# A two-block sequence model on one core: the sums behind its seven-product pairs move from POOL to DVE

## The chip, the cores and the metric

The kernel runs on one core of a Trainium2 chip. The metric is the device time of one execution in microseconds (us). The core has a matmul engine (PE, with PEld for its weight loads), a vector engine (DVE), an activation engine (ACT), a general engine (POOL, also called GpSimd) and DMA queues issued from SP. Each engine works through its own list of instructions in order and waits on semaphores of the others.

## The reference, cut to what matters

Two model blocks run one after the other on 512 tokens of width 1024 (and 256 context tokens in the second block), all in float32. The first block (an even and an odd mixer with two feed-forward parts) isn't touched by the change. The second block has two layers (`l`), each with a joint projection of the normalised tokens, three branches (`branch_a` differential attention, `branch_b` a chunked bidirectional recurrence, `branch_c` neighbourhood attention) and a gated merge:

```python
h = rms_norm(x, norm_g) * (1 + scale[:, None]) + shift[:, None]
aq, ak, av, az, bq, bk, bv, bo, bz, bg, cq, ck, cv, cz, gm = split_proj(h @ w_in)
...
g = jax.nn.sigmoid(gm.reshape(gm.shape[:2] + (N_BRANCH, -1)))
return jnp.sum(g * proj, axis=2) @ w_out
```

The gates `gm` are 3072 columns of `h @ w_in`, for 768 tokens in layer 0 and 512 in layer 1. They are where the changed code works.

## The kernel before, in words

**Matmuls in three parts.** A float32 product is made of three products of rounded parts: an operand is split by ACT (`hi`, a copy in the shorter format) and DVE (`lo`, the remainder), and `mm3` issues hi·hi, hi·lo, lo·hi. The normalised tokens stand in two resident tensors, `H` (hi) and `L` (lo). Weights arrive by DMA in `ws`, are split into `wh` by ACT and `wl` by DVE, and wait in three `ws`, four `wh` and four `wl` buffers.

**Seven-product pairs.** Two weight tiles for `gm` are multiplied with the tokens as a 2x2 block product with seven products in place of eight (`pair`, called by `gm_pair`; 12 pairs in each layer, 24 in all). That needs sums of blocks of the weights and of the tokens:

- `wpair` loads the two tiles into `ws` and makes, with four operations of 128x512, `a11-a21` (in place), `s2 = a22-a11` (in the tile `w2`, printed as `w`), `a12-s2` (in place) and `a21+a22` (in place). Between them the parts are split for the matmuls (`put`), so ACT (`wh<-w`) and DVE (`wl<-w,wh`) wait for these sums.
- `halves` runs once in each layer, at its start: for eight row tiles it adds the two parts of the tokens, `H + L`, back to float32 (128x768 in layer 0, 128x512 in layer 1; printed as `s<-H,L`), and then DVE subtracts halves of those (`s<-s`, `s<-s,s`) and splits them.

**What sets the order.** Every instruction is recorded by `Order` and issued by a planner in `flush`. It simulates the engines with costs of its own (`_cost`), takes at each step the instruction that could start first, and prefers the earlier one in the program's order among those that are ready. Its costs know the engine of an operation and nothing of what other engines do at that moment:

```python
if eng == "pool":
    return 146 + (2.1 if op == "tensor_tensor" else 3.3) * size
...
return 95 + size / (1.92 if two else 0.96)
```

Changing an operation's engine thus changes its planned cost, the planned load of two engines, and the order of everything that is planned with it. Block 2 is planned by itself, from the first `s<-H,L` on.

**Around the change.** At a layer's start `norm_lat`/`norm_ctx` write `H` and `L`; the first head of `branch_c` is prepared (`stack`: four ACT copies `s<-s 64x768`, DVE subtractions `s<-s,s 64x768`, DVE casts), and only with it can PE go on from projections to scores. In `attend` of `branch_c` and `branch_a`, DVE scales the exponentials (`s<-s,tn`), which PE then transposes (`P<-C,s`) for the product with the values.

Of the kernel before, what the change touches and what calls it, by code (L numbers as in the profile page):

```python
# [9 lines left out]
F32 = mybir.dt.float32  # L10
# [3 lines left out]
ALU = mybir.AluOpType  # L14
# [496 lines left out]
class Kern:  # L511
# [68 lines left out]
    def wpair(self, srcs):  # L580


        nc = self.nc
        self.n_ += 1
        raw = []
        for i, src in enumerate(srcs):
            st = nc.tile(self.wp, [128, 1088], F32, "wst", self.WST, f"ws{self.n_}_{i}")
            nc.sync.dma_start(out=st[:, :1024], in_=src.rearrange("p k m -> p (k m)"))
            raw.append(st)
        s2 = nc.tile(self.wp, [128, 512], F32, "w2", 1, f"w2{self.n_}")  # L590
        a11, a12, a21, a22 = (raw[i][:, 512 * j:512 * j + 512] for i in range(2) for j in range(2))
        out = {}

        def put(x, names, tags=("whi", "wlo", 1088, 4)):
            self.n_ += 1
            n = 512 * len(names)
            hi = nc.tile(self.wp, [128, tags[2]], F32R, tags[0], tags[3], f"wh{self.n_}")[:, :n]
            lo = nc.tile(self.wp, [128, tags[2]], F32R, tags[1], tags[3], f"wl{self.n_}")[:, :n]
            self.split(hi, lo, x[:, :n])
            for i, a in enumerate(names):  # L600
                out[a] = [y[:, 512 * i:512 * i + 512].rearrange("p (k m) -> p k m", k=4) for y in (hi, lo)]

        sub = lambda o, x, y: nc.gpsimd.tensor_tensor(o, x, y, op=ALU.subtract)
        put(raw[0], ("a11", "a12"))
        sub(a11, a11, a21)
        sub(s2, a22, a11)
        put(s2, ("s2",), ("w2h", "w2l", 512, 1))
        sub(a12, a12, s2)
        put(raw[0], ("s3", "s4"))
        nc.gpsimd.tensor_tensor(a21, a21, a22, op=ALU.add)  # L610
        put(raw[1], ("s1", "a22"))
        return out

# [567 lines left out]
class Block2:  # L1181
# [95 lines left out]
    def halves(self, n):  # L1277

        K, nc = self.K, self.nc
        b = self.tk = {q: [] for q in ("b11", "b21", "b22", "t1", "t2", "t3", "t4")}  # L1280
        for k in range(4):
            for nm, r, c in (("b11", k, 0), ("b21", k + 4, 0), ("b22", k + 4, n)):
                b[nm].append((K.H[:, r, c:c + n], K.L[:, r, c:c + n]))
        self.tn = n
        for k in range(4):
            x, y = self.s(2 * n), self.s(2 * n)
            for a, r in ((x, k), (y, k + 4)):
                nc.gpsimd.tensor_tensor(a, K.H[:, r, :2 * n].bitcast(F32), K.L[:, r, :2 * n].bitcast(F32), op=ALU.add)
            b11, b12, b21, b22 = x[:, :n], x[:, n:], y[:, :n], y[:, n:]
            nc.vector.tensor_tensor(b11, b12, b11, op=ALU.subtract)  # L1290
            nc.vector.tensor_tensor(b12, b22, b12, op=ALU.subtract)
            nc.vector.tensor_tensor(b22, b22, b11, op=ALU.subtract)
            nc.vector.tensor_tensor(b21, b21, b22, op=ALU.subtract)
            for a, names in ((x, ("t1", "t3")), (y, ("t4", "t2"))):
                h, l = self.ysplit(a, 2 * n)
                for i, nm in enumerate(names):
                    b[nm].append((h[:, i * n:i * n + n], l[:, i * n:i * n + n]))
            yield
# [701 lines left out]
```

## Time and profile before

| | |
|---|---|
| three timed runs | 2883.07 us median (2879.26 to 2884.18) |
| profiled execution, its own time | 2883.25 us |
| its span in the profile | 2881.5 us |
| mean granted clock of TensorE | 0.993 |
| PE busy | 2831.4 us (98%) |
| DVE busy | 2057.3 us (71%) |
| ACT busy | 1306.7 us (45%) |
| POOL busy | 393.4 us (14%), 285 instructions |

Busy time is the union of an engine's instructions. The span is the profiled program; the 1.75 us between it and the execution's own time lie around the program. The stretch before the first `s<-H,L` (at 1142 us) is block 1 and its hand-over, the 1740 us behind it are block 2. Since the engines work in order and overlap, a share of 98% on PE means that what is left to win or lose are PE's short idle stretches and the time that it runs at the lower of its two clocks.

### The profile page before, as it was taken

The numbers are of one execution on the slowest core, as the hardware profiler recorded it, in microseconds if no ns is written. First come the engines' busy times: TensorE is split into PE (matmuls) and PEld (weight loads), VectorE is DVE, ScalarE is ACT, GpSimd is POOL, SyncE is SP. The second block draws the span as 40 slices with busy tenths as digits, with TensorE's granted clock in tenths as the row PEclk, the third lists the DMA queues.
The fourth block names the chain that finished last, engine by engine and source line by source line (L and its number), as shares of the span: only waits on it lengthen the run. The fifth ranks groups of instructions, "written<-read, shape, count | busy, mean of one in ns | idle before, by whom it ended". The sixth has DMA issues, their size and how long they took to land. (4 is left out here: it accounts for less than half of the span.)

```text
span 2881.5 us, 42542 instructions
## 1 busy us (share of the span) xinstructions
PE 2831.4 (98%) x16280; PEld 2452.8 (85%) x16280; DVE 2057.3 (71%) x4049; ACT 1306.7 (45%) x2449; POOL 393.4 (14%) x285
## 2 busy tenths in 40 slices
PE   9999999999999999999999999999999999999998
PEld 7888888887888888889899989998878889989887
DVE  7878687478875875855777676575586677787765
ACT  6344234465442443754545453341256554554433
POOL 1010000010100003100211131120210121232201
PEclk9999999999999999999999999999999999999999
DMA  4333433332324423111112132254312222232362
GB/s 171 125 120 124 144 133 110 105 106 80 137 99 145 142 89 118 63 67 57 72 67 71 59 104 92 76 165 164 135 63 94 71 81 71 71 107 96 107 211 92
DMA packets 113245, 302.63 MB, mean 105 GB/s; under 512 B 11657, under 2 KB 25353, under 8 KB 113041
## 3 DMA queue, kind: packets, MB, share of 16 engines
q1 hardware_dynamic: 112896, 299.91, 30.7%
q8 instruction: 128, 2.10, 0.3%
q14 instruction: 77, 0.62, 0.1%
q10 hardware_dynamic: 144, 0.00, 0.0%
HBM read 272.26 MB, written 27.61 MB: 104 GB/s over the span
## 5 line engine op out<-in xcount | busy, mean ns | idle before, releaser
L486 PE MATMUL P<-H,wl 128*128 128x512 f32 (+2 forms) x2648 | 960.9, 363 | 4.0 <-DVE wl L486 4.0
L486 PE MATMUL P<-L,wh 128*128 128x512 f32 (+2 forms) x2648 | 961.2, 363 | 2.5 <-DVE L L486 2.5
L486 PE MATMUL P<-H,wh 128*128 128x512 f32 (+2 forms) x2648 | 960.9, 364 | 1.4 <-ACT H L486 1.4
L486 ACT ACTIVATE wh<-ws 128x1024 fp32r<-128x1024 f32 (+3 forms) x450 | 436.1, 972 | 764.3 <-PE P L486 649.1
L486 DVE TENSOR_TENSOR wl<-ws,wh 128x1024 fp32r<-128x1024 f32 (+3 forms) x450 | 523.3, 1164 | 204.3 <-ACT wh L486 202.4
L486 PEld LDWEIGHTS P<-H,wl 128*128 128x128 f32 x2648 | 500.3, 189 | 82.7 <-DVE wl L486 5.4
L486 PEld LDWEIGHTS P<-L,wh 128*128 128x128 f32 x2648 | 499.6, 189 | 83.3 <-DVE L L486 4.6
L486 PEld LDWEIGHTS P<-H,wh 128*128 128x128 f32 x2648 | 499.0, 188 | 81.4 <-ACT H L486 2.4
L486 PE MATMUL P<-s,wh 128*128 128x256 f32 (+2 forms) x1344 | 330.6, 333 | 0.0
L486 PE MATMUL P<-t,wh 128*128 128x512 f32 x960 | 301.5, 395 | 0.3 <-ACT t L486 0.3
L486 ACT ACTIVATE s<-P 128x512 f32<-128x512 f32 (+3 forms) x416 | 186.6, 482 | 222.9 <-PE P L486 202.7
L486 PE MATMUL P<-s,s 128*128 128x128 f32 (+4 forms) x1576 | 239.1, 293 | 11.9 <-DVE s L486 11.8
L486 PEld LDWEIGHTS P<-s,wh 128*128 128x128 f32 x1344 | 229.6, 189 | 17.6
L486 PEld LDWEIGHTS P<-s,s 128*128 128x128 f32 (+1 forms) x1576 | 212.8, 192 | 28.7 <-issue 10.2
L486 PE MATMUL P<-s,wl 128*128 128x256 f32 (+2 forms) x672 | 222.8, 332 | 2.1 <-DVE wl L486 2.1
L486 PEld LDWEIGHTS P<-t,wh 128*128 128x128 f32 x960 | 180.4, 188 | 43.0 <-ACT t L486 0.6
L486 ACT ACTIVATE s<-s 128x768 f32<-128x768 f32 (+7 forms) x226 | 153.3, 694 | 114.7 <-DVE s L486 97.9
L486 DVE TENSOR_TENSOR s<-s,s 128x512 f32<-128x512 f32 (+8 forms) x200 | 173.9, 875 | 26.2 <-ACT s L486 11.9
L486 PE MATMUL P<-t,wl 128*128 128x512 f32 x480 | 189.8, 395 | 0.0
L486 POOL TENSOR_TENSOR s<-s,s 128x512 f32<-128x512 f32 (+2 forms) x76 | 102.8, 1356 | 582.2 <-DVE s L486 317.7
L486 ACT ACTIVATE s<-P,tn 128x512 f32<-128x512 f32 (+1 forms) x224 | 117.8, 534 | 107.0 <-DVE tn L486 106.9
L486 ACT ACTIVATE t<-t 128x512 f32<-128x512 f32 (+4 forms) x162 | 97.5, 611 | 123.5 <-DVE t L486 122.6
(145 smaller groups left out, 3579.8 us busy)
## 6 DMA issues: line engine op xcount, KB each, us to landing
ws<-in_w2in SPq DMA_DIRECT2D x136, 512.0 KB, 3.3
ws<-in_up SPq DMA_DIRECT2D x88, 512.0 KB, 3.2
wm<-in_w_mod SPq DMA_DIRECT2D x48, 512.0 KB, 4.4
ws<-in_down SPq DMA_DIRECT2D x32, 384.0 KB, 3.1
ws<-in_w2br SPq DMA_DIRECT2D x48, 256.0 KB, 2.7
ws<-in_down SPq DMA_DIRECT2D x32, 320.0 KB, 2.9
ws<-in_w0in SPq DMA_DIRECT2D x18, 512.0 KB, 3.7
gd<-s SPq DMA_DIRECT2D x24, 384.0 KB, 2.9
```

What stands on the lines that cost most here:

```text
L486: o["f"](*o["a"], **o["k"])
```

## The change

The 96 operations of 128x512 in `wpair` and the 16 operations in `halves` (8 of 128x768, 8 of 128x512) are issued on DVE in place of POOL. Nothing else in the source is different; the planner then orders block 2 anew.

```diff
@@ wpair
-        sub = lambda o, x, y: nc.gpsimd.tensor_tensor(o, x, y, op=ALU.subtract)
+        sub = lambda o, x, y: nc.vector.tensor_tensor(o, x, y, op=ALU.subtract)
         put(raw[0], ("a11", "a12"))
         sub(a11, a11, a21)
         sub(s2, a22, a11)
         put(s2, ("s2",), ("w2h", "w2l", 512, 1))
         sub(a12, a12, s2)
         put(raw[0], ("s3", "s4"))
-        nc.gpsimd.tensor_tensor(a21, a21, a22, op=ALU.add)
+        nc.vector.tensor_tensor(a21, a21, a22, op=ALU.add)
         put(raw[1], ("s1", "a22"))
@@ halves
             for a, r in ((x, k), (y, k + 4)):
-                nc.gpsimd.tensor_tensor(a, K.H[:, r, :2 * n].bitcast(F32), K.L[:, r, :2 * n].bitcast(F32), op=ALU.add)
+                nc.vector.tensor_tensor(a, K.H[:, r, :2 * n].bitcast(F32), K.L[:, r, :2 * n].bitcast(F32), op=ALU.add)
```

The order of block 1 is the same on every engine. In block 2 three places on DVE matter here. The first is DVE at the start of layer 0, from the last `L` of the normalised tokens to the first subtractions of `stack` (`s_9672`, `s_9671`); `s_9695` and `s_9696` are the first two row tiles of `halves`, `s_9732` the third.

```order
 L486 SCALAR_TENSOR_TENSOR L<-t_2040,mod_79,H 128x512
+L486 TENSOR_TENSOR s_9695<-H,L 128x768
 L486 TENSOR_TENSOR wl_2064<-ws_2062,wh_2063 128x1024
 L486 TENSOR_TENSOR wl_2067<-ws_2065,wh_2066 128x1024
-L486 TENSOR_TENSOR wl_9799<-ws_9797,wh_9798 128x1024
+L486 TENSOR_TENSOR s_9696<-H,L 128x768
 L486 TENSOR_TENSOR s_9695<-s_9695 128x384
 L486 TENSOR_TENSOR s_9695<-s_9696,s_9695 128x384
+L486 TENSOR_TENSOR s_9696<-s_9696,s_9695 128x384
+L486 TENSOR_TENSOR s_9732<-H,L 128x768
 L486 TENSOR_TENSOR s_9672<-s_9667,s_9672 64x768
 L486 TENSOR_TENSOR s_9671<-s_9669,s_9670 64x768
```

Three of the eight sums stand ahead of `stack`'s subtractions, with one more small subtraction; the split of a later weight tile (`wl_9799`) has moved behind them, and the other five sums come later.

The second place is DVE at the first pair of layer 0, in the middle of a head's attention: `ws_0_10056` and `ws_1_10057` are the two weight tiles, `w_10058` is `s2`, `tn` are row statistics, `s_9973` and `s_9976` the exponentials being scaled.

```order
+L486 TENSOR_TENSOR ws_0_10056<-ws_0_10056,ws_1_10057 128x512
 L486 RECIPROCAL tn_9971<-tn_9971 128x2
+L486 TENSOR_TENSOR ws_1_10057<-ws_1_10057 128x512
 L486 TENSOR_SCALAR s_9973<-s_9973,tn_9971 128x512
 L486 TENSOR_SCALAR s_9976<-s_9976,tn_9971 128x512
+L486 TENSOR_TENSOR w_10058<-ws_1_10057,ws_0_10056 128x512
+L486 TENSOR_TENSOR ws_0_10056<-ws_0_10056,w_10058 128x512
+L486 TENSOR_TENSOR wl_10062<-w_10058,wh_10061 128x512
```

Two sums now stand ahead of the scaling of the exponentials and two behind it, followed at once by the split of `s2`.

The third place is DVE at the start of layer 1, at the last two `L` of the normalised tokens (`s_11572`, `s_11573` and `s_11594` belong to `halves`).

```order
+L486 TENSOR_TENSOR s_11572<-H,L 128x512
+L486 SCALAR_TENSOR_TENSOR L<-s_11518,mod_81,H 128x512
+L486 SCALAR_TENSOR_TENSOR L<-s_11519,mod_81,H 128x512
+L486 TENSOR_TENSOR s_11573<-H,L 128x512
 L486 TENSOR_TENSOR s_11572<-s_11572 128x256
 L486 TENSOR_TENSOR s_11572<-s_11573,s_11572 128x256
-L486 SCALAR_TENSOR_TENSOR L<-s_11518,mod_81,H 128x512
-L486 SCALAR_TENSOR_TENSOR L<-s_11519,mod_81,H 128x512
 L486 TENSOR_TENSOR s_11573<-s_11573,s_11572 128x256
+L486 TENSOR_TENSOR s_11594<-H,L 128x512
```

The last two `L` stood behind two subtractions of `halves`; they now stand behind one sum, and those subtractions come after them.

## Rows read from the trace of the kernel before

**Rows 1.** The page, part 1: busy us, share of the span, instructions.

```profile
PE 2831.4 (98%) x16280; PEld 2452.8 (85%) x16280; DVE 2057.3 (71%) x4049; ACT 1306.7 (45%) x2449; POOL 393.4 (14%) x285
```

**Rows 2.** Busy time by stretch: block 2 whole, then three stretches of lower PE clock.

```profile
core 0: us, PE busy (x) PEld busy (x) DVE busy (x) ACT busy (x) POOL busy (x), PEclk, DMA share, GB/s
...
1161.00:1168.00 7.00, 5.29 (x25) 5.32 (x26) 6.30 (x12) 1.07 (x2) 0.00 (x0) 0.51 0.00 0
1280.50:1284.00 3.50, 3.50 (x34) 3.17 (x31) 1.35 (x6) 2.15 (x9) 0.00 (x0) 0.51 0.02 5
...
2570.80:2577.60 6.80, 5.85 (x26) 5.68 (x27) 5.00 (x11) 5.59 (x10) 3.09 (x3) 0.50 0.11 40
1141.00:2881.00 1740.00, 1698.52 (x10971) 1534.10 (x10969) 1206.03 (x2537) 812.27 (x1717) 316.13 (x228) 0.99 0.28 94
```

**Rows 3.** PE's waits in block 2: total us, times, longest us.

```profile
PE P L486 <- DVE s L486: 21.2, 20, 4.1
```

**Rows 4.** Groups on POOL: busy us, mean ns of one, idle before.

```profile
L486 POOL TENSOR_TENSOR ws<-ws,ws 128x512 f32<-128x512 f32 x24 | 33.5, 1395 | 556.8 <-DVE wl L486 328.3 <-DVE tn L486 143.6 <-ACT s L486 65.4
...
L486 POOL TENSOR_TENSOR s<-H,L 128x768 f32<-128x768 f32 x8 | 18.1, 2294 | 34.1 <-DVE L L486 34.1
```

**Rows 5.** Groups on DVE, 1165 to 1268 us, where POOL does nothing.

```profile
L486 DVE TENSOR_TENSOR wl<-ws,wh 128x1024 fp32r<-128x1024 f32 x8 | 9.7, 1220 | 9.7 <-ACT wh L486 9.7
L486 DVE TENSOR_TENSOR s<-s,s 64x768 fp32r<-64x768 f32 x9 | 8.6, 953 | 3.0 <-ACT s L486 2.9
L486 DVE TENSOR_SCALAR s<-s,tn 128x512 f32<-128x512 f32 x18 | 7.9, 483 | 0.1
...
L486 DVE TENSOR_SCALAR s<-s,tn 128x256 f32<-128x256 f32 x8 | 2.4, 348 | 0.0
```

**Rows 6.** Groups on DVE, 216 to 432 us, where POOL does nothing either.

```profile
L486 DVE TENSOR_TENSOR t<-t,t 128x512 f32<-128x512 f32 x13 | 9.0, 690 | 0.2
```

**Rows 7.** Timeline of DVE, start of layer 0: start us, us, what, how many.

```profile
1144.32 5.28 DVE L486 TENSOR_TENSOR wl<-ws,wh 128x1024 fp32r<-128x1024 f32 x2 [2.46 <-ACT wh L486]
1151.32 2.91 DVE L486 TENSOR_TENSOR wl<-ws,wh 128x1024 fp32r<-128x1024 f32 x1 [1.72 <-ACT wh L486]
...
1156.47 5.51 DVE L486 TENSOR_TENSOR s<-s,s 128x384 f32<-128x384 f32 x3
```

**Rows 8.** Timelines of ACT and of PE at that place; in brackets idle before, releaser.

```profile
1154.93 3.30 ACT L486 ACTIVATE s<-s 64x768 fp32r<-64x768 f32 x4
...
1162.71 0.55 PE L486 MATMUL P<-s,s 128*128 128x256 f32 x1 [4.07 <-DVE s L486]
```

**Rows 9.** Timelines of DVE and of PE at the start of layer 1.

```profile
2120.71 3.10 DVE L486 SCALAR_TENSOR_TENSOR L<-s,mod,H 128x512 fp32r<-128x512 f32 x3
...
2125.71 2.06 DVE L486 SCALAR_TENSOR_TENSOR L<-s,mod,H 128x512 fp32r<-128x512 f32 x3
...
2129.01 1.46 DVE L486 TENSOR_TENSOR s<-s 128x256 f32<-128x256 f32 x1
...
2123.87 0.50 PE L486 MATMUL P<-L,wh 128*128 128x512 f32 x1 [0.70 <-DVE L L486]
...
2132.61 0.50 PE L486 MATMUL P<-L,wh 128*128 128x512 f32 x1 [1.48 <-DVE L L486]
```

**Rows 10.** Timeline of DVE beside the sums of two pairs.

```profile
1273.74 1.92 DVE L486 TENSOR_SCALAR s<-s,tn 128x512 f32<-128x512 f32 x2
...
1277.05 2.65 DVE L486 TENSOR_SCALAR s<-s,tn 128x512 f32<-128x512 f32 x2
...
1371.63 2.62 DVE L486 TENSOR_SCALAR s<-s,tn 128x256 f32<-128x256 f32 x2
```

**Rows 11.** 24 stretches: each pair's sums on POOL plus 2 us; two, the sum.

```profile
1656.70:1664.70 8.00, 8.00 (x46) 6.91 (x45) 7.97 (x10) 5.23 (x8) 5.86 (x4) 1.00 0.20 77
...
2461.80:2473.50 11.70, 11.70 (x79) 10.62 (x78) 11.48 (x18) 6.41 (x11) 9.58 (x6) 1.00 0.05 19
...
sum 196.70, PE 185.38 PEld 163.56 DVE 142.03 ACT 99.31 POOL 146.67; mean PE 7.72 PEld 6.82 DVE 5.92 ACT 4.14 POOL 6.11
```

## The prediction

> **What bounds the kernel now.** I read the page first: PE is busy for 98% of the span and DVE for 71% [rows 1]. So PE is the bound, and time can only come from, or go to, PE's idle stretches and the stretches in which its clock is low. The order of block 1 doesn't change, so I cut the trace at 1141 us. In block 2 the view by stretch gives PE 1698.5 busy of 1740 us, so 41.5 us idle, and DVE 1206 busy, so 534 us idle [rows 2]. The view of waits says for whom PE waits: the largest entry is DVE's work on `s`, 21.2 us in 20 waits [rows 3]. The same stretches show what an idle PE brings after it: behind the longest wait the granted clock is 0.51 for 7 us, which is the lower of the two levels, 1.2 in place of 2.4 GHz; two more stretches of 3.5 and 6.8 us are alike [rows 2]. What PE does in such a stretch takes twice its time, so each costs about half its length.
>
> Next I asked how long the moved operations take and what they do to others. On POOL a 128x512 sum takes 1.40 us and a 128x768 one 2.29 us [rows 4]. The third view, the timeline of DVE beside them, is the one that decides. Where POOL is idle, DVE splits a weight tile in 1.22 us and scales 128x512 exponentials in 0.48 us [rows 5]. While POOL makes its eight token sums, two such splits take 5.28 us and a third 2.91 us [rows 7]; beside a pair's sums, two scalings take 1.92, another two 2.65 us [rows 10]. DVE operations with all operands in SBUF wait for POOL's operation to end, and are counted as busy in that time. A part of DVE's 71% is therefore such waiting.
>
> **The change part by part.** *What DVE takes over.* A 128x512 operation of two SBUF operands takes 0.69 us on DVE [rows 6]. None of 128x768 on all partitions is read here; the nearest is 64x768 at 0.953 us [rows 5], which I take, since an operation's length follows its columns (0.48 and 0.35 us for 512 and 256). So: 96 x 0.69 = 66.2, 8 x 0.953 = 7.6, 8 x 0.69 = 5.5, together 79.4 us. POOL loses 112 operations and nothing waits for the rest of its work more than before.
>
> *What DVE is spared.* At the start of layer 0: three splits took 5.28 + 2.91 - 3 x 1.22 = 4.5 us too long, and the three subtractions from 1156.47 at least 5.51 - 3 x 0.953 = 2.7 us [rows 5, 7]; together 7. At the start of layer 1: three `L` took 3.10 us where three others take 2.06, and a 128x256 subtraction 1.46 us, over 0.7 us more than even a 128x512 one [rows 6, 9]; that is 1.8 shown, with six of the eight sums not counted. I take 4, between that and about 1 us for each of eight. At the pairs: two scalings and two scalings, 4.57 - 4 x 0.483 = 2.6 us at the first, 2.62 - 2 x 0.348 = 1.9 us at the second [rows 5, 10]. These are pairs where DVE had work; over the 24 pairs' stretches it is busy for 142.0 of 196.7 us, 72% [rows 11]. 2.3 x 0.72 x 24 = 40 us; the bounds are nothing, and 2.6 x 24 = 62. Spared in all: 51 us, so DVE's net gain in work is 28 us, against 534 us in which it is idle.
>
> *Start of layer 0.* PE stands for 4.07 us until `stack`'s subtractions and casts are done [rows 8]. ACT's four copies for them begin at 1154.93 and last 3.30 us, so two are ready at 1156.6; DVE was then held up, and the two subtractions are among the three operations that end at 1162.0 [rows 7]. In the new order three token sums (2.9 us), two splits (2.4) and three smaller subtractions (under 2.9) stand ahead of them, 8.2 us of work from 1141.9, where its idle time before the first split begins, to 1156.6; the cover is the 4.2 us that DVE sat idle there and the 7 us that it lost. So they begin with ACT's copies: 1156.6 + 2 x 0.953 for the subtractions, and the 0.7 us after which PE went on, is 1159.2, not 1162.7. PE's wait shrinks by 3.5 us, to 0.6. The low clock behind it cost half of 7 us; whether 0.6 us of idleness still brings it the rows don't tell, so I take half of that, 1.7.
>
> *Start of layer 1.* PE waits for `L` for 0.70 and 1.48 us [rows 9]. The first is the `L` lengthened by POOL. The second stands behind two lengthened subtractions; in the new order one 0.69 us sum replaces them. I count both as gone: 2.2 us.
>
> *The pairs.* In the 24 stretches PE is idle for 196.7 - 185.4 = 11.3 us [rows 11], and two of the low-clock stretches lie at pairs and cost half of 10.3 us, 5.1 [rows 2]. The waits are for operations like the lengthened scalings. But the four sums now take 2.8 us of DVE themselves, two of them ahead of the scaling at the first pair: 1.4 us in place of the 2.6 lost. I therefore take half of both: 5.7 and 2.6 us.
>
> *What is late next.* DVE has 28 us more to do, and behind a sum in its queue stand statistics, scalings and splits for which PE waits. At the present ratio (41.5 us of PE idle to 1206 of DVE busy) that would be 1 us of PE; if none of it fell into DVE's gaps, 28 us. A planner that lays out block 2 anew also moves what has nothing to do with the sums. I take 3.5 us, near the lower end, since in most of the 24 stretches PE doesn't wait at all.
>
> A rule against the change is in the Trainium skill, page Perfetto Trace Analysis, section Optimizing Scalar/DVE Operations: a saturated DVE may be relieved by giving work to ScalarE or even GpSimd, though between DVE and GpSimd this may not help, because they share a read port of SBUF. By its first half the sum would be the slower rival's below, by its second half about no change; rows 7 and 10 agree with the shared port, and no row says that DVE is saturated over block 2.
>
> *Sum.* 3.5 + 1.7 + 2.2 + 5.7 + 2.6 - 3.5 = 12.2 us less. The profiled execution took 2883.25 us by its own clock, 0.2 us from the median of the runs. Forecast: 2871 us.
>
> **The rivals.** *The gain is spent where it is made (no change).* DVE's own sums take 2.8 us a pair where POOL's held it up by 1.7 on average (40 of 24). If the planner puts them ahead of what PE waits for, as with two of four at the first pair, PE's 11.3 us and the low clock stay. Then the two starts (7.4 us as forecast) stand against 28 us of added work, of which a quarter reaching PE cancels them: 2877.5 to 2889, say 2882. For it: only three of the waits that I shorten were opened. Against: the starts are not at pairs.
>
> *DVE becomes the late one (slower).* There are pair stretches in which DVE is full: 7.97 of 8.0 and 11.48 of 11.7 us, and PE didn't wait in either [rows 11]. There a pair's sums push everything behind them back by 2.8 us less what is spared, 1.1 us net; that lies on the softmax chain of scores, statistics, scaling and transposes. If half of the 28 us arrives at PE, and nothing else is won, it is 2883 + 14 = 2897. It decides as soon as more than 21.5 us of lateness reach PE while the gains are as forecast (15.7 us, and 5.8 us that a measurement can tell), or 5.8 us if they fail. Against it: these full stretches are full partly because of the waits on POOL, which go.
>
> *More is won.* All of the pairs' idle time and clock goes as well, and all of the first low-clock stretch, with no new wait: 3.5 + 3.5 + 2.2 + 11.3 + 5.1 = 25.6 us, 2858.
>
> **How the numbers follow.** Chances: forecast with gains between 6 and 20 us 0.50, more won 0.10, no change 0.25, slower 0.15. A difference under 0.2%, 5.8 us, is about what a measurement of this kernel can't tell from none. It counts the first two cases as faster: faster 0.60, same 0.25, slower 0.15. The likeliest case alone has 2863 to 2877. The range must leave out no more than 2 in 10: its low end is the case in which all is won, 2857 with a us of margin; its high end takes in the whole no-change case and the near part of the slower one, 2890. The predicted time is that of the likeliest case, 2871 us.
>
> **What would show it.** Right: DVE's splits at the start of layer 0 at 1.22 us each, the scalings beside a pair at 0.48 us, PE's wait of 4.07 us under 1.5, no wait for `L` at layer 1, block 2's PE idle near 32 us in place of 41.5, DVE's busy time up by 20 to 35 us, not by 79. Wrong: DVE up by the full 79 (nothing was spared); PE waits for `s` and `tn` as long as now but at other instructions (the first rival); new waits for `wl` or statistics right behind the moved sums, or more stretches at half clock (the second). The step that I hold weakest is the half taken at the pairs, then the 3.5 us for what is late next.

## The result, and the profile after

The changed kernel takes 2854.32 us (median of 4 runs, 2853.95 to 2855.64), the kernel before 2881.99 us in runs beside it: ratio 0.9905, 95% interval 0.9888 to 0.9922. The gain is 27.7 us, where 12.2 were forecast; the time lies 3 us below the low end of the range. The profiled execution of the kernel after has a span of 2853.5 us.

The page of the kernel after, part 1, answers to [rows 1]:

```profile
PE 2823.1 (99%) x16280; PEld 2446.9 (86%) x16280; DVE 2058.9 (72%) x4161; ACT 1307.3 (46%) x2449; POOL 230.7 (8%) x173
```

Read DVE and POOL together. POOL lost 163 us of work, DVE got 112 operations, and DVE's busy time rose by 1.6 us. The groups on DVE of the kernel after show that the new operations do take what was assumed, and that the scalings beside them are back at their undisturbed price:

```profile
L486 DVE TENSOR_SCALAR s<-s,tn 128x512 f32<-128x512 f32 x64 | 28.2, 482 | 0.7
L486 DVE TENSOR_TENSOR ws<-ws,ws 128x512 f32<-128x512 f32 x24 | 16.5, 687 | 0.3
L486 DVE TENSOR_TENSOR wl<-w,wh 128x512 fp32r<-128x512 f32 x24 | 16.5, 686 | 1.4 <-ACT wh L486 1.4
L486 DVE TENSOR_TENSOR s<-H,L 128x768 f32<-128x768 f32 x8 | 7.5, 952 | 0.1
L486 DVE TENSOR_TENSOR s<-H,L 128x512 f32<-128x512 f32 x8 | 5.5, 683 | 0.0
```

So 79 us of new work came, and all but 1.6 us of it was given back: DVE had lost some 78 us in waits beside POOL's 112 operations (estimate: 79.4 - 1.6), 0.69 us for each.

Busy time by stretch in the kernel after, to be read beside [rows 2] (same columns): three stretches of low clock, and block 2 whole.

```profile
1166.00:1172.80 6.80, 5.77 (x16) 4.61 (x17) 6.63 (x26) 5.68 (x23) 0.00 (x0) 0.50 0.01 4
1684.80:1688.20 3.40, 3.40 (x13) 3.20 (x14) 3.37 (x8) 2.28 (x3) 0.00 (x0) 0.50 0.39 155
2548.40:2551.80 3.40, 3.37 (x15) 2.91 (x14) 2.81 (x8) 1.76 (x3) 0.00 (x0) 0.50 0.40 154
1141.00:2853.50 1712.50, 1689.85 (x10969) 1528.56 (x10968) 1207.89 (x2649) 813.12 (x1716) 153.84 (x116) 0.99 0.28 95
```

Block 2 is 27.5 us shorter. PE is idle for 1712.5 - 1689.85 = 22.7 us of it, not 41.5, which is 18.8 us; and PE is busy for 8.7 us less with the same matmuls. The second part is mostly the clock. The kernel before had, besides the three stretches in [rows 2], three more in block 2, each of 3.4 us at the lower level:

```profile
1697.00:1700.40 3.40, 3.40 (x13) 3.40 (x14) 3.02 (x5) 0.85 (x1) 3.28 (x2) 0.50 0.30 116
1707.20:1710.60 3.40, 3.40 (x15) 3.40 (x14) 3.05 (x5) 3.40 (x12) 0.93 (x1) 0.50 0.15 41
2154.40:2157.80 3.40, 3.40 (x17) 3.30 (x17) 2.54 (x11) 1.05 (x4) 0.00 (x0) 0.50 0.02 5
```

That is some 27 us at half clock before and 13.6 after, the tail of the program apart; half of the difference, some 7 us, is the clock's share of PE's busy time in these two executions. It isn't the same in every execution: the mean granted clock of the kernel before is 0.993 in the profiled one and 0.995 on average over 60 others (0.993 to 0.996), that of the kernel after 0.996 to 0.997, so the usual share is nearer 4 us (estimate: 0.0013 of the span).

PE's waits in block 2 of the kernel after (total us, times, longest us), the first of them beside [rows 3]:

```profile
PE P L486 <- DVE s L486: 8.8, 10, 2.6
PE P L486 <- ACT s L486: 3.3, 2, 3.0
PE P L486 <- DVE wl L486: 2.2, 2, 2.0
PE P L486 <- issue: 1.2, 1, 1.2
```

**Where along the program.** PE has the same number of matmuls in both kernels, so the start of its n-th matmul can be compared. The gain is 0.3 us at the 5300th (end of block 1, 1138.3 us in the kernel before), 1.5 at the 5900th (1234.2, behind the start of layer 0), 15.7 at the 11300th (2087.7, end of layer 0), 23.5 at the 11900th (2194.0, behind the start of layer 1) and 27.9 at the last. So: start of layer 0 1.2 us, the rest of layer 0, where its pairs are, 14.2, start of layer 1 7.8, the rest of layer 1 4.4. (These are single executions, one of each kernel.)

*Start of layer 0.* DVE and then PE in the kernel after, beside [rows 7, 8]:

```profile
1144.03 1.23 DVE L486 TENSOR_TENSOR wl<-ws,wh 128x1024 fp32r<-128x1024 f32 x1 [1.42 <-ACT wh L486]
1145.66 1.23 DVE L486 TENSOR_TENSOR wl<-ws,wh 128x1024 fp32r<-128x1024 f32 x1 [0.41 <-ACT wh L486]
...
1155.48 1.93 DVE L486 TENSOR_TENSOR s<-s,s 64x768 fp32r<-64x768 f32 x2 [5.21 <-ACT s L486]
1157.45 1.02 DVE L486 CAST s<-s 64x768 fp32r<-64x768 f32 x2
...
1167.03 0.79 PE L486 MATMUL P<-H,wh 128*128 128x512 f32 x1 [2.95 <-ACT s L486]
```

The splits take 1.23 us and `stack`'s subtractions begin with ACT's copies, as forecast, and the wait of 4.07 us is gone. But from 1164 us PE now waits for ACT for 2.95 us, and from 1166 us the clock is at 0.50 for 6.8 us.

*Start of layer 1.* Busy time in 40 us around the last `L`, in the kernel before and in the kernel after (same columns):

```profile
2118.00:2158.00 40.00, 34.81 (x164) 27.92 (x162) 37.59 (x60) 23.89 (x36) 12.69 (x8) 0.96 0.12 41
```

```profile
2105.00:2145.00 40.00, 39.97 (x215) 33.19 (x215) 38.09 (x92) 30.27 (x60) 0.00 (x0) 1.00 0.17 60
```

Before, PE is idle there for 5.2 us and the clock is not full; after, both are gone. Two of the waits are those of [rows 9]; the third, which no term of mine counted, is this:

```profile
2153.32 2.69 PE L486 MATMUL P<-s,s 128*128 128x256 f32 x15 [2.98 <-DVE s L486]
```

### The profile page after: what moved, and what is told of

Same layout as the page of the kernel before. It is cut to its first block, busy times and chain, and to the rows that moved or that the text cites. A ratio compares the mean times of both kernels' runs of the same rounds, so it can differ in the third digit from the quotient of the medians.

```text
span 2853.5 us, 42462 instructions
## 1 busy us (share of the span) xinstructions
PE 2823.1 (99%) x16280; PEld 2446.9 (86%) x16280; DVE 2058.9 (72%) x4161; ACT 1307.3 (46%) x2449; POOL 230.7 (8%) x173
## 4 chain that ended last, share of the span: by engine, by line
PE 94%; DVE 3%; ACT 2%; DMA 1%; issue 0%; SPq 0%; POOL 0%; DVEq 0%; ACTq 0%; POOLq 0%
PE P L486 92%; DVE s L486 2%; ACT s L486 1%; PE P L488 1%; DVE wl L486 1%; DMA s<-cmd 0%; ACT t L486 0%; DVE t L486 0%; ACT wh L486 0%; DMA X<-in_x 0%; DVE tn L486 0%; SPq L486 0%; ACT H L486 0%; DVE ws L486 0%; DMA cmd<-s 0%
## 5 line engine op out<-in xcount | busy, mean ns | idle before, releaser
L486 DVE TENSOR_TENSOR wl<-ws,wh 128x1024 fp32r<-128x1024 f32 (+3 forms) x450 | 507.9, 1130 | 200.2 <-ACT wh L486 196.0
L486 DVE TENSOR_TENSOR s<-s,s 128x512 f32<-128x512 f32 (+8 forms) x200 | 166.9, 839 | 27.1 <-ACT s L486 16.0
```

The lines of the kernel that those rows point to most:

```text
L486: o["f"](*o["a"], **o["k"])
```

## The experiments

Fourteen more kernels were run; the kernel before took 2880.9 to 2882.4 us (medians) beside them. "Gain" is against that. The table has those that part the engine from the order; the others follow it.

| sums | planner charges them to | us | gain | ratio, 95% interval |
|---|---|---|---|---|
| POOL | POOL (before) | 2882 | | |
| POOL | POOL, 60 ns more | 2881.4 | 0.8 | 0.9998 (0.9989 to 1.0006) |
| POOL | POOL, true price | 2888.2 | -6.6 | 1.0020 (1.0011 to 1.0029) |
| POOL | POOL, short price | 2897.3 | -15.7 | 1.0053 (1.0040 to 1.0065) |
| POOL | DVE | 2869.8 | 12.6 | 0.9959 (0.9946 to 0.9971) |
| POOL | DVE, true price | 2870.1 | 12.1 | 0.9960 (0.9947 to 0.9974) |
| DVE | POOL | 2862.5 | 19.9 | 0.9929 (0.9916 to 0.9941) |
| DVE | DVE (after) | 2854.3 | 27.7 | 0.9905 (0.9888 to 0.9922) |
| DVE | DVE, true price | 2855.6 | 26.0 | 0.9908 (0.9895 to 0.9922) |

**Which of the sums.** Each half of the change alone.

```diff
 pairs only: wpair's four operations on nc.vector, halves' stays on nc.gpsimd
 tokens only: halves' operation on nc.vector, wpair's stay on nc.gpsimd
```

> Only the 96 sums of the weights are done on DVE; the 16 sums of the tokens stay on POOL. If the gain is made of DVE time that was lost beside POOL, it divides by place: most of the 27.7 us comes with the pairs, 15 to 20 us, so 2862 to 2867 us, DVE's busy time about 15 us above that of the kernel with all sums on DVE less their own 11 us, and the two waits at the starts of the layers (4.07 us, and 0.70 + 1.48 us for L) are back. If it is a lucky new order, nothing divides: anything from 2855 to 2882 us, and this run and the one with the tokens' sums alone don't add up to 27.7 us.

> Only the 16 sums of the tokens are done on DVE; the 96 sums of the weights stay on POOL. Lost DVE time: 8 to 12 us of the gain are made at the starts of the two layers, so 2870 to 2874 us, and the scalings beside the first pair take about twice 0.48 us as before. New order: anything from 2855 to 2882 us.

Measured: pairs only 2864.3 us (ratio 0.9938, 0.9926 to 0.9951), tokens only 2872.2 us (0.9965, 0.9952 to 0.9979). The gains, 18.1 and 10.2 us, add up to 28.3 where the whole change gave 27.7, so the gain divides by place. By the count of matmuls the tokens' sums alone gain the same 7.8 us at the start of layer 1 as the whole change (2.2 us at the 11300th, 10.0 at the 11900th), and the pairs' alone nothing there (12.8, 12.7).

**Engine or order.** The change moves the operations and also lets the planner lay block 2 out anew. The two can be parted, since what the planner is told and what is issued need not be the same engine.

```diff
+self.asif = _Engine(self, "pool", nc.vector)   # on DVE, planned as POOL's
+self.asif = _Engine(self, "dve", nc.gpsimd)    # on POOL, planned as DVE's
-nc.gpsimd.tensor_tensor(...)
+nc.asif.tensor_tensor(...)
```

In the first, PE, ACT and SP keep the order of the kernel before and DVE has the sums put into its old order; in the second they have the order of the kernel after.

> All 112 sums are done on DVE, but the planner still costs and places them as POOL's work, so PE, ACT, SP keep the order of the kernel before and DVE has the sums put into its old order. Lost DVE time, or sums that are ready sooner: most of the gain is there, 20 us or more, 2855 to 2862 us, and DVE's busy time stays within 10 us of 2057. New order: nothing is gained, 2878 to 2886 us, or some us more than before, since DVE has 79 us of work that no plan knows of.

> All 112 sums are done on POOL, but the planner costs and places them as DVE's work, so PE, ACT, SP have the order of the kernel after. New order: most of the gain is there, 2855 to 2862 us. Lost DVE time, or sums that come late: nothing is gained, 2876 to 2890 us, and the sums of DVE's and POOL's busy times are near those of the kernel before (2057 and 393).

Measured: 2862.5 us and 2869.8 us. Neither theory has it all: the engine alone gives 19.9 us, the order alone 12.6, both 27.7, so 4.8 us are won by either. The pages, part 1, of the two (DVE in the old order first):

```profile
PE 2822.6 (99%) x16280; PEld 2445.8 (85%) x16280; DVE 2063.1 (72%) x4161; ACT 1307.0 (46%) x2449; POOL 229.9 (8%) x173
```

```profile
PE 2822.1 (98%) x16280; PEld 2443.2 (85%) x16280; DVE 2057.2 (72%) x4049; ACT 1308.0 (46%) x2449; POOL 392.7 (14%) x285
```

In these executions PE's busy time is down by some 9 us in both, as in the kernel after; the rest is idle time (span less busy): 50.1 us before, 45.9 with the order alone, 38.7 with the engine alone, 30.4 with both. The two sums can trade places: the run "POOL, 60 ns more" of the table, no faster than the kernel before, has PE busy for 2826.1 us, 5.3 less, and idle for 3.6 us more. So how much of each gain is the clock's isn't shown. DVE's busy time is the same in all four within 6 us, with the sums on it or not. So the gain isn't less busy time on DVE, nor, by the runs further down, sums that are ready sooner. What is left is where in DVE's queue the time falls.

The first pair shows it. DVE with POOL's sums in the new order; in the kernel before the same operations take the same times to within 0.04 us [rows 10]:

```profile
1272.76 1.20 DVE L486 TENSOR_TENSOR wl<-ws,wh 128x1024 fp32r<-128x1024 f32 x1
1273.88 1.91 DVE L486 TENSOR_SCALAR s<-s,tn 128x512 f32<-128x512 f32 x2
1275.72 1.23 DVE L486 TENSOR_TENSOR tn<-tn 128x2 f32<-128x2 f32 x1
1276.98 0.17 DVE L486 RECIPROCAL tn<-tn 128x2 f32<-128x2 f32 x1
1277.18 2.69 DVE L486 TENSOR_SCALAR s<-s,tn 128x512 f32<-128x512 f32 x2
```

The same stretch in the kernel after:

```profile
1271.09 1.21 DVE L486 TENSOR_TENSOR wl<-ws,wh 128x1024 fp32r<-128x1024 f32 x1
1272.21 0.88 DVE L486 TENSOR_SCALAR s<-s,tn 128x512 f32<-128x512 f32 x2
1273.00 0.15 DVE L486 TENSOR_TENSOR tn<-tn 128x2 f32<-128x2 f32 x1
1273.07 0.68 DVE L486 TENSOR_TENSOR ws<-ws,ws 128x512 f32<-128x512 f32 x1
1273.67 0.16 DVE L486 RECIPROCAL tn<-tn 128x2 f32<-128x2 f32 x1
1273.79 0.69 DVE L486 TENSOR_TENSOR ws<-ws 128x512 f32<-128x512 f32 x1
1274.40 0.88 DVE L486 TENSOR_SCALAR s<-s,tn 128x512 f32<-128x512 f32 x2
1275.19 0.68 DVE L486 TENSOR_TENSOR w<-ws,ws 128x512 f32<-128x512 f32 x1
1275.91 0.69 DVE L486 TENSOR_TENSOR ws<-ws,w 128x512 f32<-128x512 f32 x1
```

From the split's end to the end of the second scalings DVE takes 5.9 us with the sums on POOL (1273.96 to 1279.87) and 3.0 us with two of them in between on DVE (1272.30 to 1275.28). POOL's sums hold most of what DVE wants to do next, here the scalings and the small `tn` operation between them (1.23 us in place of 0.15; the reciprocal behind it isn't held); of DVE's own sums two stand behind what PE waits for. The order's part shows on PE. The kernel before, and then the new order with the sums on POOL:

```profile
1276.19 0.47 PE L486 MATMUL P<-L,wh 128*128 128x512 f32 x1
1278.44 0.63 PE L486 MATMUL P<-C,s 128*128 128x128 f32 x4 [1.78 <-DVE s L486]
1279.85 0.52 PE L486 MATMUL P<-C,s 128*128 128x128 f32 x3 [0.78 <-ACT s L486]
```

```profile
1276.33 0.48 PE L486 MATMUL P<-L,wh 128*128 128x512 f32 x1
1276.65 0.40 PE L486 MATMUL P<-H,wl 128*128 128x512 f32 x1
...
1277.84 1.80 PE L488 MATMUL P<-s,s 128*64 128x128 f32 x29
1279.58 1.09 PE L486 MATMUL P<-C,s 128*128 128x128 f32 x8
```

DVE is as late in both. But a plan that charges the sums to DVE knows that the scalings will be late, and gives PE other matmuls first: the transposes (`P<-C,s`) then start without a wait.

**The charge, or a lucky order.** The planner's price of the sums was varied with the engines left alone (a few lines: the planned cost is raised or lowered behind each recorded sum).

> The kernel before, with its sums on POOL, but the planner counts them as long as they took there (1400 in place of 1221 ns for 128x512, 2294 in place of 1759 for 128x768). If any other order of block 2 is better than that of the kernel before, 2868 to 2876 us, as with the order planned for DVE. If that order is better because it charges the sums to DVE's queue, which they do hold up, a truer price on POOL brings nothing: 2878 to 2887.

> The kernel before, with its sums on POOL and planned on POOL, but at the price that the planner gives them on DVE (628 and 895 ns). It parts the two things that the order planned for DVE has: a short price, and the charge to DVE's queue. If the short price makes that order better, 2867 to 2873 us; if the charge does, 2878 to 2890.

> The kernel after, with the planner's prices of the sums on DVE as they took (687 in place of 628 ns, 953 in place of 895). It is a small push on the order, which says how far an order as such moves the time: if the order of the kernel after is no lucky one, 2851 to 2858 us; if it is, 2860 us or more.

> All sums on POOL, but costed and placed as DVE's work, at the prices they take there (687 and 953 ns): the order of the run with DVE's true prices, a second order that charges DVE's queue. If the charge makes such an order better, 2866 to 2874 us, as the first one (2869.8). If that one was luck, 2878 to 2895 us, as the orders that charge POOL.

> All sums on POOL and placed as POOL's work, with 60 ns more in the planner's price of each: one more order that charges POOL, near that of the kernel before. If the charge is what matters, 2878 to 2897 us, where the other three such orders lie. If the orders scatter by luck, anything from 2866 us on.

Measured (the table): with the sums on POOL, the four orders that charge POOL lie at 2881 to 2897 us, the two that charge DVE both at 2870; with the sums on DVE, the second order is within 1.3 us of the first. A short price without the charge is the worst of all. The two POOL orders at a true and at a short price came out 1 and 7 us above the ranges that I gave if the charge is what matters, on the side away from a gain. So a price alone isn't what makes the order better, and the charge to DVE is what the better orders share. Luck isn't wholly excluded: they are two orders against four, the two differ by 59 ns in the price, and orders do scatter, since three other prices on POOL moved the time by 1, 7 and 16 us.

**Sums that are ready sooner, or DVE's load.** The kernel after with each of the 96 sums of weights done twice on DVE, all orders kept; in the second run the spare one stands ahead.

```diff
 twice:        real sum, then vector.tensor_tensor(idle, o, a22)
 spare first:  vector.tensor_tensor(idle, x, y), then real sum
```

> The kernel after, with each of the 96 sums of weights followed by one more of the same shape on DVE into a scratch tile: 66 us of DVE work that spares nothing, with POOL idle as in the kernel after and the order of all else the same. If DVE has room, the time rises by 1 to 4 us, to 2855 to 2858, which is the size of my term for what is late next. If DVE's load itself reaches PE, by a quarter of 66 us, to about 2871 us; then the gain of the change can only be explained with the 78 us that DVE was spared.

> As the run with each sum of weights done twice on DVE, but the spare one stands ahead of the real one, so each real sum is ready 0.69 us later at the same load of DVE, 2.8 us for the four of a pair, about what POOL's 1.40 us each came to. If the change won because the sums are ready sooner, this is 8 us or more above the 2881.9 us of that run. If it won because DVE's other operations are no longer held up, or by the order, the moment at which the sums are ready is worth little: within 4 us of 2881.9.

Measured: 2881.9 us (2879.8 to 2887.4) and 2880.5 us (2875.1 to 2884.0). At this load of DVE, sums that are ready 0.69 us later each cost nothing; that theory falls. But the load cost more than either figure that I had given, 1 to 4 us or some 17: DVE's busy time rose by 62.9 us and the time by 27.5, 0.44 us for each us of DVE, when the plan doesn't know of it.

**POOL operations that nobody needs.** The kernel after, and behind each sum of weights one more on POOL, into a scratch tile; all orders kept. In the second run it is a copy.

```diff
 sums:    real sum on DVE, then gpsimd.tensor_tensor(idle, o, a22)
 copies:  real sum on DVE, then gpsimd.tensor_copy(idle, o)
```

> The kernel after, with 96 operations on POOL that nobody needs: behind each sum of weights on DVE, POOL adds its result and a quarter of a weight tile into a scratch tile, 128x512 in float32, as the old sums were. Every engine's order is that of the kernel after. Lost DVE time: DVE's busy time rises by 40 to 60 us though it has no new work, and the time goes back by 10 to 20 us, to 2864 to 2874. If the gain came from sums that are ready sooner, or from the new order: no change, 2853 to 2857 us, and DVE within 5 us of 2059.

> As the run with POOL operations that nobody needs behind each sum, but POOL copies the sum (one operand in SBUF) in place of adding two. If any POOL operation on SBUF holds DVE up, DVE's busy time rises by 30 us or more and the time goes back by 8 us or more, to 2862 or more. If it takes POOL operations of two operands in SBUF, neither moves: 2853 to 2857 us, DVE within 8 us of 2059.

Measured: 2898.2 us with the sums (ratio to the kernel before 1.0061, 1.0048 to 1.0073), 2861.6 us with the copies. The groups of the run with sums:

```profile
L486 DVE TENSOR_TENSOR s<-P,s 128x384 f32<-128x384 f32 x84 | 45.7, 553 | 16.5 <-PE P L486 15.0 <-ACT s L486 0.8
L486 DVE TENSOR_REDUCE tn<-P 128x1 f32<-128x512 f32 x64 | 43.6, 682 | 1.9 <-PE P L486 1.7
L603 POOL TENSOR_TENSOR idle<-ws 128x512 f32<-128x512 f32 x24 | 38.9, 1622 | 5.8 <-DVE ws L603 4.2
L486 DVE TENSOR_TENSOR wl<-w,wh 128x512 fp32r<-128x512 f32 x24 | 32.5, 1353 | 0.0
```

The split of `s2`, right behind a sum, takes 1353 ns where it took 686. The groups that read `P` (PSUM) are as long as in the kernel after (the first of them 553 ns, there 552), but few of them lie beside a bystander; two of the 84 in the first group began while one ran, and took 557 and 558 ns. DVE's busy time rose from 2058.9 to 2144.3 us without new work, 0.89 us for each bystander, more than the 0.66 that a sum costs DVE when it does it itself (62.9 us over 96); the time rose by 44 us. Both are about twice what I expected. That is the kernel after made slower than the kernel before by POOL operations that nobody needs. Not all of the 44 us need be DVE's: PE's waits for DVE's `s` and `wl` grew from 11.0 to 35.0 us, and it waits 6.7 us for POOL's other work, which it didn't before. Late weights aren't the cause: ACT waits 4.3 us for `ws`, 0.8 in the kernel after. Copies cost DVE 0.32 us each (2089.5 us busy) and 7 us of time. They hold DVE too, so an operation on POOL needn't have two operands to do so; the time stayed 0.4 us under the bound that I gave.

**The rest of POOL's work too.** All of POOL's other operations of two operands, in both blocks, on DVE, planned so (twelve further lines, nc.gpsimd to nc.vector).

> The kernel after, with all of POOL's other operations of two operands (about 161, 230 us on POOL) on DVE too, in both blocks, planned so. Lost DVE time: DVE gets about 130 us of work at its own prices and is spared the 42 us that it still loses beside POOL, so its busy time rises by 80 to 90 us to about 2145; what PE can win is less than the 30 us that it is still idle; 2846 to 2854 us. Rival: the load of DVE is what PE waits for now, and the time rises to 2860 or more.

Measured: 2849.2 us, ratio to the kernel before 0.9888 (0.9875 to 0.9902), the fastest of all, with DVE at 2118.4 us:

```profile
PE 2821.1 (99%) x16280; PEld 2445.6 (86%) x16280; DVE 2118.4 (74%) x4322; ACT 1308.3 (46%) x2449; POOL 1.1 (0%) x12
```

DVE's busy time rose by 59 us, less than the 80 to 90 that I expected, and the time fell by 5; by the count of matmuls nearly all of this is block 1 (5.1 us sooner at the 5300th, 0.3 in the kernel after). About as much more busy time on DVE cost 27 us in the run with sums done twice, which no plan knew of, and nothing here, where it was planned. That the plan makes the difference isn't shown by this pair: the operations are others, at other places, and POOL's are gone.

## Why the prediction was too small

**Right.** The mechanism: DVE waits beside POOL's operations, the sums on DVE give it that time back, PE's stalls behind DVE shrink, and the clock recovers with them. The prices on DVE (687 and 952 ns against 690 and 953), the splits at 1.23 us, the scalings at 0.48 us and no wait for `L` at layer 1 were as said; PE's idle time in block 2 fell too, to 22.7 us where some 32 were forecast. One premise is too wide: not every operation with all operands in SBUF waits for POOL (the last section has the exceptions). The slower rival and the no-change rival are both refuted by 27.7 us. The rival in which more is won, 2858 us, came within 4 us, but not by its terms: it had the start of layer 1 at 2.2 us, and the first low-clock stretch gone.

**The step that failed** is the one named as the weakest: the half taken at the pairs. 8.3 us were forecast there (5.7 idle, 2.6 clock); 18.6 were measured by the count of matmuls (14.2 + 4.4, all of both layers but their starts), more than the whole that I had counted, 16.4. By the same count the engine alone gives 15.8 us there and the order alone 9.8, so the half was too small even for the part of it that I had reasoned about. I had weighed 1.4 us of sums ahead of the scalings against 2.6 us lost on the scalings. The rows show that the small `tn` operation between them lost 1.1 us as well, and that the stretch as a whole went from 5.9 to 3.0 us with both sums in it. And the cut of 24 stretches, "each pair's sums plus 2 us", was too narrow: 13.6 us of PE's idle time in block 2 of the kernel before lie outside them, the two starts and the time behind the last matmul. Of the three further low-clock stretches shown above, which the sum left out, one lies inside one of the 24 (at 1697.0 us) and one 2 us behind it.

**Other terms.** The start of layer 1 gave 7.8 us, not 2.2: I counted two waits for `L` and left out the third, 2.98 us for `stack`'s casts, with 3.4 us at half clock behind it. It is the same wait as at layer 0, one layer on. The order alone removes it too: with the sums on POOL in the new order no wait of PE over 1 us is left there, and 3.8 us are gained; with the sums on DVE in the old order one of 1.29 us stays, and 3.2 us are gained. The start of layer 0 gave 1.2 us, not 5.2: the wait of 4.07 us went, but one of 2.95 us for ACT came with the new order, and the low clock stayed. The runs in the new order with the sums on POOL (2.99 us), or done twice (2.96), have this wait too; the old order with the sums on DVE has one of 1.76 us for DVE in its place. So the wait belongs to the order; the low clock behind it doesn't always come, since in the run with the sums on POOL the granted clock there is 1.00. The 3.5 us for what is late next can't be found in the total. The four errors are 10.3 + 5.6 - 4.0 + 3.5 = 15.4 us, which is the miss of 15.5 (27.7 - 12.2) to within 0.1.

**DVE spared:** 51 us were counted, with an upper bound of 62 for the pairs; it was 78. Beside POOL not only scalings and splits are held, but also small `tn` operations that I had priced at nothing. That DVE's busy time would rise by 20 to 35 us is a sign that failed. The net gain in DVE's work was not 28 but 1.6 us, which made the forecast of new lateness too high.

**What I had not thought of** is that the order carries a part by itself. I wrote that a planner which lays out block 2 anew moves what has nothing to do with the sums, and put a loss on it. It is a gain: 12.6 us with the sums on POOL, 7.8 more with the sums on DVE (27.7 - 19.9). I read it as having to do with the sums: a plan that puts them on POOL takes DVE for free where it is held, while one that charges DVE (628 ns each, where 0.69 us are lost) is nearly true, on whichever engine the sums are. The two orders that charge DVE fit that; they don't prove it.

The Trainium skill, page Perfetto Trace Analysis, section Optimizing Scalar/DVE Operations, which the prediction weighed, says in its second half that moving work from DVE to GpSimd may not help, since they share a read port. The traces agree as far as DVE's time goes: 0.69 us of DVE were lost for each sum on POOL, against 0.69 us to do it. "About no change" of the kernel's time, which I had made of it, was wrong by 27.7 us: DVE's total stayed, but the time now falls elsewhere in its queue.

What stays open: how the 20 us of the engine part divide over the single pairs (the first was shown; for the others only the sum is known), and what part of the gain is the clock's.

## What to carry to other kernels

An operation of two SBUF operands on POOL isn't off DVE's books: before giving POOL such work, compare DVE's busy time with and without it, and look at whatever DVE does beside it, the smallest operations too. If an order is planned by costs, try charging a POOL operation to DVE's queue; in this kernel that gave 12.6 us with the sums left on POOL. And when waits repeat from layer to layer, cost each of the repeats, with the low clock that may come behind it.

## What the runs showed of the hardware

- How long DVE is held: 0.69 us for a POOL sum in the kernel before (estimate: 78 us over 112), 0.89 us for a bystander right behind a DVE sum, 0.32 us for a one-operand copy of the same size. The Trainium skill, page SBUF — State Buffer, section SBUF: two separate sides, has the two engines share one pair of ports by an exclusive lock, which the one that starts first holds for a whole instruction; on DVE's side it names operations with two inputs in SBUF and those in a two-port mode. The trace agrees: a 128x2 `tn` operation of 0.15 us took 1.23 us beside POOL's sums, and operations with an operand in PSUM aren't held. The nine `s<-P,V,s` of 128x511 that began while a bystander sum ran took 740 ns, 749 where POOL did nothing.
- Not every operation on SBUF alone is held. In the run with the sums on POOL in the new order, four reductions (`tn<-s`, 128x512 to 128x4) lie beside a pair's sum; they took 677 to 687 ns, the four others 676 to 687.
- POOL's 128x512 sum took 1.40 us in the kernel before [rows 4] and 1.62 us (`idle<-ws`) in the run with bystander sums, where DVE operations follow each other closely. No run was made to show whether DVE holds POOL in turn.
- The low clock doesn't follow every wait. At the start of layer 0 PE waits 2.95 us for ACT in the kernel after, and the clock is 0.50 for 6.8 us; the same wait took 2.99 us in the run with the sums on POOL in the new order and 2.93 us with copies, and the clock behind it was 1.00 in both.
